# A hybrid recurrence-and-attention block: the second weight sum of three projection units is put behind two splits, and the next unit's first block behind one more load

## The chip, the core and the metric

The kernel runs on one core of a Trainium2 chip. The metric is the device time of one execution in microseconds (us), lower is better. The matrix engine TensorE is PE in the profile, the weight loads that overlap its matmuls are PEld, VectorE is DVE, ScalarE is ACT, GpSimd is POOL and SyncE is SP. SP issues the large loads on a queue of its own (SPq), POOL issues DMAs on another one.

## The reference, cut to what matters

```python
def rms_norm(x, w):
    y = x * lax.rsqrt(jnp.mean(x * x, axis=-1, keepdims=True) + EPS)
    return y * w

# x: (1, 256, 2048), all float32; one layer
z = rms_norm(h, norm_mix_w) @ w_in                       # 2048 x 11264
hq, hf, hi, hg, aq, ak, av, gates = jnp.split(z, ...)
y_a = hgrn2(hq, hf, hi, hg)                              # 8 heads of 128, gated recurrence over time
y_b = chunk_band_attention(aq, ak, av, rel_bias)         # 16 heads of 64, bias by relative distance
gate_a, gate_b = jnp.split(sigmoid(gates), 2)
merged = gate_a * (y_a @ w_branch_a) + gate_b * (y_b @ w_branch_b)
h = h + merged @ w_out
h = h + square(relu(rms_norm(h, norm_mlp_w) @ w_up)) @ w_down
return rms_norm(h, norm_final_w)
```

There are 256 tokens, so every weight is used once per token block and the work is a long row of matrix products with 256 rows.

## The kernel before, in words

**Arithmetic.** Products are made to float32 accuracy from two rounded parts of each operand. A weight piece is 128 x 1024 float32 (512 KB). ScalarE casts it into a high part (`wh`, line 91), VectorE subtracts that from the raw piece to get the low part (`wl`, line 92), and PE runs three matmuls, high by high, high by low, low by high (lines 135, 136 and 137, helper `mm3`). The function `parts` does the cast and the subtraction and appends the subtraction to the list `lows`. High and low parts sit in rings of four buffers each, and of five once the list `homes` has an entry "fifth", which is from the unit ga2 on. Instructions of a line in a helper all show that line, so tiles tell the units apart.

**Units.** A `Unit` makes a 256 x 1024 slice of a product with a 2048-deep contraction. Half of the depth (rows 0 to 7 of 16) is done with seven block products in place of eight, after Strassen and Winograd. The weight half has four blocks A, B, C, D of two pieces each. They are split and multiplied in this order: 11 with A, 22 with A, 12 with C, 11 with D, a plain piece, 21 with A, a plain piece, 21 with B, two plain pieces, 21 with D, plain pieces. Between them the blocks are changed in place: `sums("A","B")` adds B to A on VectorE (line 780) after the first product, `sums("A","C")` adds C to A before the 21 product with A, and `sent` makes POOL issue DMAs that add C to B and the changed A to D in SBUF (line 785). A DMA of `sent("D","A")` needs its D piece to have been split and its A piece to have been summed.

**Plain pieces.** The other half of the depth is eight plain pieces, `(n, (k, k+1))`, n being the column half. They are loaded into three buffers `rawp` in the order of `ITEMS`: (1,8), (1,10), (0,8), (0,10), and so on. So the fourth one, (0, (10, 11)), can be loaded only when the first one, (1, (8, 9)), has been split. The last two plain pieces of column half 1 are late: they are put into the list `late` and run inside the next unit, between its first products.

**Which units.** The projection uses `av` (attention values), `ga0` and `ga2` (first gate), `gb0` and `gb2` (second gate); later units are the output projection and the MLP. `alone` runs a unit and flushes its late pieces at once. It is called for `av` and for `ga0`, with `ga2` as the unit that follows `ga0`. So `av`, `ga0` and `ga2` begin with no late pieces in front of their second and third products, all others with two.

**Order.** The program is written as a list. A scheduler then places the instructions on each engine by priorities and estimated times; `tc.high_priority` pulls an instruction ahead, and `tc.issue_after(x)` keeps those in its block behind x. Every engine and every DMA queue then runs its list in order and waits where a semaphore is not yet there. The scores, the softmax and the value products of the attention (lines 587 to 626) are placed between the matmuls of units: those of the first eight heads start during `av`, those of the other eight run during `ga0`. In these, PE has three kinds of short float32 work: `s` (scores, 64-row operands, line 587), `tpp` (transposes of 128 x 128, line 610) and `pa` (value products, 64 columns, line 622). The pool of `s` has one buffer. During `ga0` the units' accumulators in PSUM are halves of pair tiles; from `ga2` on each one is a bank of its own.

**Lines named below.** 91 cast, 92 low part, 135 to 137 matmuls, 587 scores, 596 and 597 scores plus bias, 599 and 600 maxima, 606 and 607 scaling, 610 transposes, 688 loads of pieces, 123 loads of the qk projection's weights, 748 copies of an accumulator (`u`, and the start of one accumulator from another), 775 subtraction of `u`, 780 `sums`, 785 `sent`.

Before the change `sums("A","C")` is held behind the latest low part only in units made with `fresh=True`, which are `ga2` and `gb0`; in all units `then.load("A")` stands behind the copy `u1`:

```python
        u.product("11", "D", u.block(0, 1))
        with ExitStack() as es:
            if u.fresh:
                es.enter_context(tc.issue_after(lows[-1].ins))
            u.sums("A", "C")
        u.sent("D", "A")
        ...
        u1 = u.copy(token(f"u1_{u.what}"), "21")
        if then:
            then.load("A")
```

Of the kernel before, what the change touches and what calls it, by code (L numbers as in the profile page):

```python
# [22 lines left out]
NC = 512  # L23
# [10 lines left out]
C_HI, C_HG, C_AV = 0, HG, 2 * HG  # L34
# [16 lines left out]
def tile_hybrid_block(  # L51
# [5 lines left out]
    nc = tc.nc  # L57
# [42 lines left out]
    def new_act(what):  # L100

        return apool.tile([P, 4, 2, T], F32R, name=f"act_{what}", tag="act")
# [96 lines left out]
    xT = [new_act(f"x{c}") for c in range(4)]  # L199
# [3 lines left out]
    steps = [1, 1] + [2] * (KD // 2 - 1)  # L203
# [10 lines left out]
    done = [0, 0]  # L214
    for kt, n in zip(starts, steps):
        c, a = kt // 4, kt % 4
# [361 lines left out]
    def qk_chunk(col, what, factor, acc=None):  # L578
        return z_t(col, what, bp.tile([P, 2, T], F32, name=f"{what}T", tag="qk", bufs=6), factor, acc)
# [46 lines left out]
    def token(what, pool=None):  # L626
        if pool is not None:
            return pool.tile([P, NC], F32, name=what, tag="t2", bufs=8)
        return tk.tile([P, NC], F32, name=what, tag="t", bufs=TOK)

    def sigmoid(gate, acc, m):
        with tc.high_priority(offset=2000):
            nc.scalar.activation(gate, acc, AF.Sigmoid, scale=rstd[:, m:m + 1])
        return gate
# [46 lines left out]
    def piece(w, what, n0, k0, tag="raw"):  # L681

        pool, bufs = {"raw": (wpool, 6), "rawd": (xp, 2), "rawp": (xp, 3)}[tag]
        raw = pool.tile([P, 2 * NC], F32, name=f"{tag}_{what}", tag=tag, bufs=bufs)
        ncols = w.shape[-1]
        kpr = 4 * NC // ncols
        src = w[n0 // ncols:(n0 + NC) // ncols, k0 // kpr, :, k0 % kpr:k0 % kpr + 2, :].rearrange("c p a n -> p c a n")
        nc.sync.dma_start(raw.rearrange("p (c a n) -> p c a n", a=2, n=ncols), src)
        return raw, ncols < NC

    lows = []

    def parts(raw, what):

# [12 lines left out]
    def bank(what):  # L707
        if "banks" in homes:
            return homes["banks"].tile([P, NC], F32, name=f"acc_{what}", tag="k")
        row, col = what[-2:]  # L710
        if col not in pairs:
            pairs[col] = new_acc(what)
        return pairs[col][:, int(row) - 1, :]
# [6 lines left out]
    ITEMS = [(1, (8, 9)), (1, (10, 11)), (0, (8, 9)), (0, (10, 11)), (0, (12, 13)), (0, (14, 15))] + [(1, ks) for ks in LATE]  # L720

    class Unit:


        def __init__(self, lhs, S, w, n0, what, done, kt0=0, steps=lambda: (), start=5, fresh=False, tail=False):
            self.lhs, self.S, self.w, self.n0, self.what, self.done = lhs, S, w, n0, what, done
            self.kt0, self.make_steps, self.start, self.fresh, self.tail = kt0, steps, start, fresh, tail
            self.raw, self.c, self.items, self.steps = {}, {}, list(ITEMS), []

        def load(self, name):  # L730

# [4 lines left out]
        def load_item(self):  # L736

            n, ks = self.items.pop(0)
            self.raw[n, ks] = piece(self.w, f"{self.what}r{n}_{ks[0]}", self.n0 + n * NC, self.kt0 + ks[0], "rawp")

        def bank(self, i):

# [74 lines left out]
    def flush():  # L817
        while late:
            late.pop(0)()

    def run(u, then=None):

        def q():
            if late:
                late.pop(0)()

        def item(x):
            if x and x.items:
                x.load_item()

        if not u.raw:
            u.load("A")
            u.load("B")
            u.load("C")
            u.load("D")
        for _ in range(3 - sum(type(k) is tuple for k in u.raw)):
            item(u)
        at = iter(range(99))
        u.bank("11")
        u.product("11", "A", u.block(0, 0), True)  # L840
        u.begun("21", "11")
        q()
        u.sums("A", "B")
        u.sent("B", "C")
        item(u)
        u.bank("22")
        u.product("22", "A", u.comb(5), True)
        u.begun("12", "22")
        q()
        item(u)  # L850
        u.steps = list(u.make_steps())
        u.step(next(at))
        u.product("12", "C", u.comb(4))
        u.step(next(at))
        u.product("11", "D", u.block(0, 1))
        with ExitStack() as es:
            if u.fresh:
                es.enter_context(tc.issue_after(lows[-1].ins))
            u.sums("A", "C")
        u.sent("D", "A")  # L860
        u.step(next(at))
        u.plain(1, (8, 9))
        item(u)
        u.step(next(at))
        u.product("21", "A", u.comb(2))
        u1 = u.copy(token(f"u1_{u.what}"), "21")
        if then:
            then.load("A")
        u.step(next(at))
        u.plain(1, (10, 11))  # L870
        u.less("12", u1)
        item(u)
        u.step(next(at))
        u.product("21", "B", u.comb(7))
        u2 = u.copy(token(f"u2_{u.what}"), "21")
        if then:
            then.load("B")
            then.load("C")
        u.step(next(at))
        u.plain(0, (8, 9))  # L880
        u.less("22", u2)
        item(u)
        u.step(next(at))
        u.plain(0, (10, 11))
        item(u)
        u.step(next(at))
        u.product("21", "D", u.block(1, 1))
        if then:
            then.load("D")
        u.step(next(at))  # L890
        u.plain(0, (12, 13))
        item(u)
        u.step(next(at))
        u.plain(0, (14, 15))
        marks.clear()
        item(then)
        u.end(0)
        while u.steps:
            u.step(99)

        if u.tail:
            halves = [u.plain(1, ks, ()) for ks in LATE]
            for m, c in ((1, slice(0, T)), (0, slice(0, NC)), (1, slice(T, NC))):
                for h in halves:
                    h(m, c)
                u.done(m, 1, u.c["12"[m] + "2"], c)
            return

        def rest():
            u.plain(1, LATE[1])  # L910
            u.end(1)

        late.append(lambda: u.plain(1, LATE[0]))
        late.append(rest)


    Sx = {}
    for f in combos(xT, "x", tk, Sx):
        f()
    av = [[None] * NM for _ in range(2)]  # L920
# [5 lines left out]
    def alone(u, then=None):  # L926
        run(u, then)
        flush()
        pairs.clear()

    for g in range(2):
        qT = [qk_chunk(C_AQ + g * NC + i * T, f"aq{g}{i}", rstd8_t, None if g else acc_q[i]) for i in range(2)]
        kT = [qk_chunk(C_AK + g * NC + i * T, f"ak{g}{i}", rstd_t) for i in range(2)]
        if not g:
            alone(Unit(lambda: xT, lambda: Sx, w_in_n, C_AV, "av", values))
        yb.append(new_act(f"yb{g}"))
        pts = None
        for pr in range(5):
            last = pts
            if pr < 4:  # L940
                pts = attn_pair(g, pr, qT[pr // 2][:, pr % 2, :], kT[pr // 2][:, pr % 2, :])
            if last:
                attn_values(g, pr - 1, last, av[g])

    ga, gb = [], []
    units = []
    for gates, c, col, what, fresh in ((ga, 0, C_GA, "ga", False), (ga, 2, C_GA, "ga", True), (gb, 0, C_GB, "gb", True), (gb, 2, C_GB, "gb", False)):

        def done(m, n, acc, gates=gates, c=c, what=what):
            while len(gates) <= c + n:  # L950
                gates.append([None] * NM)
            gates[c + n][m] = sigmoid(token(f"gate_{what}{c + n}{m}", tkb if (what == "ga") == (c == 2) else None), acc, m)

        units.append(Unit(lambda: xT, lambda: Sx, w_in_t, col + c * NC, f"{what}{c}", done, fresh=fresh))
    alone(*units[:2])
    del units[0]
    bpool_cm.__exit__(None, None, None)
# [20 lines left out]
    for u, then in zip(units, units[1:] + [None]):  # L978
        run(u, then)
# [76 lines left out]
    def h_out(m, n, acc):  # L1056
        t = token(f"h1_{n}_{m}")
        with tc.high_priority(offset=2000):
# [9 lines left out]
    units = [Unit(lambda: mT, lambda: Sm, w_out, n0 * NC, f"wo{n0}", lambda m, n, acc, n0=n0: h_out(m, n0 + n, acc),  # L1068
                  steps=(lambda: h_blocks(0)) if n0 else (lambda: turned(mT, 3, "m3", ga)), start=2 if n0 else 0) for n0 in (0, 2)]
    fin = {}  # L1070
    for qd in range(NQ):
# [18 lines left out]
        for c in range(0, 4, 2):  # L1090
            def done(m, n, acc, c=c, rs=rs, qd=qd):
                t = token(f"r{qd}{c}{n}{m}")
                with tc.high_priority(offset=2000):
# [5 lines left out]
                              steps=(lambda turns=turns: turns(0)) if c else (lambda: ()) if qd else (lambda: h_blocks(2)), start=3 if c else 0))  # L1099
# [39 lines left out]
        for n0 in (0, 2):  # L1139
            units.append(Unit(lambda uT=uT: uT, lambda Su=Su: Su, w_down, n0 * NC, f"dn{qd}{n0}",  # L1140
                              lambda m, n, acc, *c, n0=n0, out_of=out_of: out_of(m, n0 + n, acc, *c), kt0=qd * KD,
                              steps=(lambda: ()) if n0 else (lambda turns=turns, last=last: turns(2) + [(3, finals)] * last),
                              start=0, tail=last and n0 == 2))

    for u, then in zip(units, units[1:] + [None]):
        run(u, then)
# [44 lines left out]
```

## Time and profile before

| | |
|---|---|
| median of 3 runs | 1399.73 us (1399.07 to 1400.38) |
| profiled execution, its own time | 1399.67 us |
| its span in the trace | 1398.0 us |
| mean granted TensorE clock | 0.998 |
| instructions | 18644 |
| read from HBM, written | 271.67 MB, 10.49 MB |

The profile is one execution. Its own time is 1.7 us more than its span, and 0.06 us under the median of the runs. In a timeline row the first number is the start in us from the beginning of the span, the second how long the row's instructions took together; what stands in square brackets is the idle time of the engine before it and what ended it. Rows of SPq and of POOL's DMA lines show the issue of a transfer and not its landing. In the chain of waits each row is a piece of the path that ended last, with its start, its length and what held it.

### The profile page before, as it was taken

The numbers are of one execution on the slowest core, as the hardware profiler recorded it, in microseconds if no ns is written. First come the engines' busy times: TensorE is split into PE (matmuls) and PEld (weight loads), VectorE is DVE, ScalarE is ACT, GpSimd is POOL, SyncE is SP. The second block draws the span as 40 slices with busy tenths as digits, with TensorE's granted clock in tenths as the row PEclk, the third lists the DMA queues.
The fourth block names the chain that finished last, engine by engine and source line by source line (L and its number), as shares of the span: only waits on it lengthen the run. The fifth ranks groups of instructions, "written<-read, shape, count | busy, mean of one in ns | idle before, by whom it ended". The sixth has DMA issues, their size and how long they took to land.

```text
span 1398.0 us, 18644 instructions
## 1 busy us (share of the span) xinstructions
PE 1381.4 (99%) x6550; PEld 1144.4 (82%) x6550; DVE 1138.2 (81%) x1431; ACT 922.3 (66%) x1192; POOL 143.8 (10%) x228
## 2 busy tenths in 40 slices
PE   9999999999999999999999999999999999999997
PEld 7889888878777888888888888888888888888885
DVE  7897997976978785687998987889877888879885
ACT  6774764665676674346777776778666876668764
POOL 2000001010100000001211001100011001010200
PEclk9999999999999999999999999999999999999999
DMA  9755455775769897658988889998899888999883
GB/s 318 242 168 161 154 166 181 225 269 162 183 187 271 251 278 225 193 169 268 283 244 275 252 268 267 274 280 240 249 295 299 248 230 254 281 279 275 267 245 114
DMA packets 124078, 331.62 MB, mean 237 GB/s; under 512 B 11072, under 2 KB 11840, under 8 KB 123600
## 3 DMA queue, kind: packets, MB, share of 16 engines
q1 hardware_dynamic: 103264, 264.80, 55.1%
q0 software_dynamic: 19568, 64.04, 23.3%
q10 hardware_dynamic: 1152, 1.60, 0.4%
q8 instruction: 51, 0.84, 0.2%
q14 instruction: 43, 0.35, 0.1%
HBM read 271.67 MB, written 10.49 MB: 202 GB/s over the span
## 4 chain that ended last, share of the span: by engine, by line
PE 90%; DVE 4%; DMA 3%; issue 1%; ACT 1%; POOL 0%; SPq 0%; POOLq 0%; ACTq 0%; DVEq 0%
PE acc_ak L177 2%; PE acc_aq L177 2%; PE acc_hf L177 2%; PE ps L414 1%; PE acc_ak L182 1%; PE acc_hq L177 1%; PE tp_u L108 1%; PE acc_ga0c L135 1%; PE acc_hg L136 1%; PE acc_bb L136 1%; PE acc_hg L135 1%; PE acc_ba L136 1%; PE acc_bb L137 1%; PE acc_ba L137 1%; PE acc_hg L137 1%
## 5 line engine op out<-in xcount | busy, mean ns | idle before, releaser
L177 PE MATMUL acc_hf<-act_x,wh_hf 128*128 128x512 f32 x128 | 41.0, 402 | 1.0 <-DVE f L190 1.0
L177 PE MATMUL acc_aq<-act_x,wh_aq 128*128 128x512 f32 x128 | 41.6, 406 | 0.0
L177 PE MATMUL acc_hq<-act_x,wh_hq 128*128 128x512 f32 x128 | 40.7, 399 | 0.0
L177 PE MATMUL acc_ak<-act_x,wh_ak 128*128 128x512 f32 x128 | 40.0, 396 | 0.1
L91 ACT CAST wh_bb<-raw_bb 128x1024 fp32r<-128x1024 f32 x16 | 16.9, 1054 | 23.3 <-PE acc_ba L137 17.7
L92 DVE TENSOR_TENSOR wl_bb<-raw_bb,wh_bb 128x1024 fp32r<-128x1024 f32 x16 | 19.6, 1223 | 14.8 <-ACT wh_bb L91 14.8
L91 ACT CAST wh_ba<-raw_ba 128x1024 fp32r<-128x1024 f32 x16 | 16.8, 1052 | 20.9 <-PE acc_bb L137 13.8
L92 DVE TENSOR_TENSOR wl_ba<-raw_ba,wh_ba 128x1024 fp32r<-128x1024 f32 x16 | 19.6, 1223 | 12.6 <-ACT wh_ba L91 12.6
L91 ACT CAST wh_aq<-raw_aq 128x1024 fp32r<-128x1024 f32 x16 | 16.8, 1050 | 19.0 <-PE acc_hg L137 8.8
L92 DVE TENSOR_TENSOR wl_aq<-raw_aq,wh_aq 128x1024 fp32r<-128x1024 f32 x16 | 19.6, 1223 | 11.4 <-ACT wh_aq L91 9.4
L182 PEld LDWEIGHTS acc_hq<-act_x,wl_hq 128*128 128x128 f32 x128 | 23.4, 188 | 6.1 <-DVE wl_hq L92 0.9
L182 PEld LDWEIGHTS acc_hf<-act_x,wl_hf 128*128 128x128 f32 x128 | 23.4, 188 | 6.1 <-DVE wl_hf L92 0.9
L182 PEld LDWEIGHTS acc_aq<-act_x,wl_aq 128*128 128x128 f32 x128 | 23.5, 188 | 5.4 <-issue 0.5
L182 PEld LDWEIGHTS acc_ak<-act_x,wl_ak 128*128 128x128 f32 x128 | 23.5, 188 | 5.3
L92 DVE TENSOR_TENSOR wl_hf<-raw_hf,wh_hf 128x1024 fp32r<-128x1024 f32 (+2 forms) x21 | 20.3, 967 | 7.8 <-ACT wh_hf L91 7.7
L91 ACT CAST wh_hf<-raw_hf 128x1024 fp32r<-128x1024 f32 (+1 forms) x19 | 16.9, 890 | 14.3 <-PE acc_hg L137 6.0
L182 PE MATMUL acc_aq<-act_x,wl_aq 128*128 128x256 f32 x128 | 25.9, 284 | 0.0
L92 DVE TENSOR_TENSOR wl_ak<-raw_ak,wh_ak 128x1024 fp32r<-128x1024 f32 x16 | 19.5, 1221 | 7.7 <-ACT wh_ak L91 7.7
L135 PE MATMUL acc_hi<-wh_hi,act_x 128*128 128x512 f32 x64 | 25.8, 403 | 0.0
L92 DVE TENSOR_TENSOR act_u<-tp_u,act_u 128x512 fp32r<-128x512 f32 x32 | 21.9, 685 | 4.7 <-ACT act_u L91 4.2
L135 PE MATMUL acc_hg<-wh_hg,act_x 128*128 128x512 f32 x64 | 25.7, 401 | 0.0
L1106 POOL DMA_DIRECT2D hd<-y x24 | 25.4, 1137 | 1.9 <-ACT y L1105 1.8
(1922 smaller groups left out, 5248.0 us busy)
## 6 DMA issues: line engine op xcount, KB each, us to landing
raw_hi<-in_w_in_n_dram SPq DMA_DIRECT2D x16, 512.0 KB, 4.4
raw_hg<-in_w_in_n_dram SPq DMA_DIRECT2D x16, 512.0 KB, 3.9
raw_aq<-in_w_in_t_dram SPq DMA_DIRECT2D x16, 512.0 KB, 4.3
raw_ak<-in_w_in_t_dram SPq DMA_DIRECT2D x16, 512.0 KB, 3.8
raw_ba<-in_w_branch_a_dram SPq DMA_DIRECT2D x16, 512.0 KB, 4.5
raw_bb<-in_w_branch_b_dram SPq DMA_DIRECT2D x16, 512.0 KB, 4.6
raw_hf<-in_w_in_t_dram SPq DMA_DIRECT2D x12, 512.0 KB, 3.9
raw_hq<-in_w_in_t_dram SPq DMA_DIRECT2D x12, 512.0 KB, 4.4
```

Source lines behind the costliest of these rows:

```text
L91: casts[:] = [(copy or nc.scalar.copy)(hi, src)]
L92: return nc.vector.tensor_tensor(lo, src, hi.bitcast(F32), op=ALU.subtract)
L108: nc.tensor.transpose(tp[:, j, :], src[:, j * P:(j + 1) * P], ident)
L135: nc.tensor.matmul(acc, hi, wh, start=first, stop=False, skip_group_check=True)
L136: nc.tensor.matmul(acc, hi, wl, start=False, stop=False, skip_group_check=True)
L137: nc.tensor.matmul(acc, lo, wh, start=False, stop=last, skip_group_check=True)
L177: nc.tensor.matmul(acc[:, cb, :], wh[:, cb * P:(cb + 1) * P], r.rearrange("p u t -> p (u t)"), start=kt == 0, stop=last)
L182: nc.tensor.matmul(acc[:, cb, 0:T], wl[:, cb * P:(cb + 1) * P], r[:, 0, :], start=False, stop=False)
L414: nc.tensor.matmul(ps[:, m, :], klf[:, a * P:(a + 1) * P], qrf[:, a * 192:(a + 1) * 192], start=True, stop=True)
L1106: nc.gpsimd.dma_start(hd[n][m], t, accum_op=ALU.add)
```

## The change

The change gives `Unit` a flag `lone`, set for `av`, `ga0` and `ga2`. In such a unit `sums("A","C")` is issued behind the last low part made so far, which is that of the second piece of D, so the order on VectorE is the splits of C and D first and the two additions then. `ga2` already had that from `fresh`. The load of the next unit's block A is issued behind the load of the plain piece (0, (10, 11)) of the unit itself; only `ga0` and `ga2` have a next unit at that place. To be able to name that load, `piece` keeps its last DMA in the list `loads` and `load_item` files it under the piece's name.

```diff
-        nc.sync.dma_start(raw.rearrange("p (c a n) -> p c a n", a=2, n=ncols), src)
+        loads[:] = [nc.sync.dma_start(raw.rearrange("p (c a n) -> p c a n", a=2, n=ncols), src)]
...
-    lows = []
+    lows, loads = [], []
...
-        def __init__(self, lhs, S, w, n0, what, done, kt0=0, steps=lambda: (), start=5, fresh=False, tail=False):
+        def __init__(self, lhs, S, w, n0, what, done, kt0=0, steps=lambda: (), start=5, fresh=False, lone=False, tail=False):
...
             self.raw[n, ks] = piece(self.w, f"{self.what}r{n}_{ks[0]}", self.n0 + n * NC, self.kt0 + ks[0], "rawp")
+            self.dma[n, ks] = loads[0]
...
         with ExitStack() as es:
-            if u.fresh:
+            if u.fresh or u.lone:
                 es.enter_context(tc.issue_after(lows[-1].ins))
             u.sums("A", "C")
         u.sent("D", "A")
...
         if then:
-            then.load("A")
+            with ExitStack() as es:
+                if u.lone:
+                    es.enter_context(tc.issue_after(u.dma[0, (10, 11)].ins))
+                then.load("A")
...
-            alone(Unit(lambda: xT, lambda: Sx, w_in_n, C_AV, "av", values))
+            alone(Unit(lambda: xT, lambda: Sx, w_in_n, C_AV, "av", values, lone=True))
...
-        units.append(Unit(lambda: xT, lambda: Sx, w_in_t, col + c * NC, f"{what}{c}", done, fresh=fresh))
+        units.append(Unit(lambda: xT, lambda: Sx, w_in_t, col + c * NC, f"{what}{c}", done, fresh=fresh, lone=what == "ga"))
```

In the built programs the order of PE's instructions differs in `ga0` alone, where the attention of the last eight heads is placed anew among the unit's matmuls; in `av` and `ga2` it is the same. VectorE's and ScalarE's orders differ in `ga0`, and VectorE's in `av` by the place of the two additions. The number of instructions is the same on every engine. On SP the load of (0, (10, 11)) moves ahead of two loads of the next unit in `ga0` and `ga2`, and later plain pieces move ahead of the next unit's blocks B, C and D; in `av` two plain pieces move ahead of one load each of the qk projection. On POOL, in `ga0`, two loads of bias and their two memsets move ahead of the `sent` from A to D.

More of the change, by code (lines that the diff above doesn't have):

```diff
@@ L722, in tile_hybrid_block @@
     class Unit:
-        def __init__(self, lhs, S, w, n0, what, done, kt0=0, steps=lambda: (), start=5, fresh=False, tail=False):
+        def __init__(self, lhs, S, w, n0, what, done, kt0=0, steps=lambda: (), start=5, fresh=False, lone=False, tail=False):
             self.lhs, self.S, self.w, self.n0, self.what, self.done = lhs, S, w, n0, what, done
-            self.kt0, self.make_steps, self.start, self.fresh, self.tail = kt0, steps, start, fresh, tail
-            self.raw, self.c, self.items, self.steps = {}, {}, list(ITEMS), []
+            self.kt0, self.make_steps, self.start, self.fresh, self.lone, self.tail = kt0, steps, start, fresh, lone, tail
+            self.raw, self.dma, self.c, self.items, self.steps = {}, {}, {}, list(ITEMS), []
         def load(self, name):
```

## The prediction

> **What bounds the kernel now.** I read the page first, then PE's waits, the chain of waits, and the timelines of the three units that the change touches.
>
> ```profile
> span 1398.0 us, 18644 instructions
> PE 1381.4 (99%) x6550; PEld 1144.4 (82%) x6550; DVE 1138.2 (81%) x1431; ACT 922.3 (66%) x1192; POOL 143.8 (10%) x228
> ```
>
> PE is busy in 99% of the span. An edit that moves no PE work can win only PE's idle time, 16.6 us in all, and the slow places inside its busy time; it can lose without limit by a new wait. In PE's waits one row of over half a us lies in the units that change:
>
> ```profile
> PE acc_ga2c L135 <- ACT u_ga L748: 1.1, 1, 1.1
> ```
>
> The bound of 0.2% used below, about what a measurement of this kernel can tell from no change, is 2.8 us. The idle time in reach is less than that.
>
> **ga2: the late fourth piece.** The chain of waits shows what stands behind the 1.1 us:
>
> ```profile
> 425.97 1.15 DVE wl_ga2r L92
> 427.13 10.89 DMA rawp_ga2r<-in_w_in_t_dram
> 439.05 1.63 ACT wh_ga2p21D L91 x2
> 440.94 0.58 ACT u_ga L748
> 441.57 0.50 PE acc_ga2c L135
> 442.07 0.23 PE acc_ga2c L136
> ```
>
> The piece (0, (10, 11)) is issued at 427.13, as soon as the first plain piece is split, and lands 10.89 us later, at 438.02. ScalarE's queue holds behind its cast two casts of D and the copy `u`, and PE must not overwrite the copied accumulator before 441.53. The stall is 1.1 us idle and a restart of 0.50 instead of 0.23, so 1.4 us. Without it PE would come to this matmul at about 440.3. From landing to matmul the chain takes 441.57 - 438.02 = 3.55, so a landing by 436.75, 9.6 us after issue, hides all of it.
>
> Why 10.9 us: two loads of the next unit stand ahead of it in the same queue, and the two `sent` transfers from A to D are in flight.
>
> ```profile
> 424.89 1.50 SPq L688 DMA_DIRECT2D raw_gb0A<-in_w_in_t_dram  x2
> 427.13 0.37 SPq L688 DMA_DIRECT2D rawp_ga2r<-in_w_in_t_dram  x1
> ```
>
> The change puts the piece first. Its issue can't come earlier, since its buffer comes free when the split of the chain's first row ends (425.97 + 1.15), but nothing stands ahead of it. The nearest rows are two fourth pieces that were issued with both `sent` transfers in flight and no load of the last 3 us still ahead of them, in ga0 and av (each answer: the issue, then the landing):
>
> ```profile
> L688 SPq DMA_DIRECT2D rawp_ga0r<-in_w_in_t_dram x1: 367/367/367, 373.1 to 373.1; - x1
> DMA to landing us min/median/max: 8.0/8.0/8.0
> L688 SPq DMA_DIRECT2D rawp_avr<-in_w_in_n_dram x1: 328/328/328, 273.0 to 273.0; - x1
> DMA to landing us min/median/max: 8.5/8.5/8.5
> ```
>
> 8.0 to 8.5 is under 9.6, so the stall goes: -1.4 us (bounds -1.4 and 0, if the landing stays at 10.9). What is late next is the pieces (0, (12, 13)) and after; they too move ahead of gb0's blocks on SP, and gb0's A, moved back by 1 us, is not cast before ga2's own pieces are.
>
> **av: the same lateness is brought in.** Here the additions were early; now they come behind D's splits.
>
> ```profile
> 261.81 1.22 DVE L780 TENSOR_TENSOR raw_avA<-raw_avA,raw_avC 128x1024 f32<-128x1024 f32 x1
> 265.54 1.22 DVE L92 TENSOR_TENSOR wl_avp12C<-raw_avC,wh_avp12C 128x1024 fp32r<-128x1024 f32 x1
> 266.68 1.22 DVE L780 TENSOR_TENSOR raw_avA<-raw_avA,raw_avC 128x1024 f32<-128x1024 f32 x1
> 267.81 1.22 DVE L92 TENSOR_TENSOR wl_avp12C<-raw_avC,wh_avp12C 128x1024 fp32r<-128x1024 f32 x1
> 268.95 2.35 DVE L92 TENSOR_TENSOR wl_avp11D<-rawd_avD,wh_avp11D 128x1024 fp32r<-128x1024 f32 x2
> 271.79 1.23 DVE L92 TENSOR_TENSOR wl_avr<-rawp_avr,wh_avr 128x1024 fp32r<-128x1024 f32 x1 [0.48 <-ACT wh_avr L91]
> ```
>
> PE gains nothing from the earlier splits, it runs this stretch without a wait. What moves is the DMA. Each raw buffer of C has two last readers, the split and the addition; in before the split is last, and SP issues the first two loads of the qk projection into these buffers right behind the two splits (266.76 and 269.03):
>
> ```profile
> 266.79 2.60 SPq L123 DMA_DIRECT2D raw_aq<-in_w_in_t_dram  x2
> 273.04 0.33 SPq L688 DMA_DIRECT2D rawp_avr<-in_w_in_n_dram  x1
> ```
>
> Afterwards the addition is last. With one addition less ahead of them, D's low parts end at about 270.7, the additions at 271.8 and 273.0, the first plain piece's low part at 274.1 (each 1.14 from start to start, as above). So the two raw_aq loads are issued at 271.8 and 273.0, the `sent` transfers at about 272.1 and 273.2, and the fourth piece at 274.1. That is ga2's pattern of before to a quarter of a us: loads 2.24 and 1.10 us ahead, transfers in flight. Two such pieces were measured, 10.9 us in ga2 and this one in gb0, also behind two loads:
>
> ```profile
> 466.05 1.51 SPq L688 DMA_DIRECT2D raw_gb2A<-in_w_in_t_dram  x2
> ```
>
> ```profile
> L688 SPq DMA_DIRECT2D rawp_gb0r<-in_w_in_t_dram x1: 368/368/368, 468.4 to 468.4; - x1
> DMA to landing us min/median/max: 10.1/10.1/10.1
> ```
>
> 10.1 to 10.9 puts the landing at 284.2 to 285.0. When is it needed?
>
> ```profile
> 282.71 1.05 ACT L91 CAST wh_avr<-rawp_avr 128x1024 fp32r<-128x1024 f32 x1 [1.18 <-PE acc_avc L137]
> 284.07 1.06 ACT L91 CAST wh_avp21D<-rawd_avD 128x1024 fp32r<-128x1024 f32 x1 [0.30 <-PE acc_avc L137]
> 285.43 0.58 ACT L748 COPY u_av<-acc_avc 128x512 f32<-128x512 f32 x1 [0.30 <-PE acc_avc L137]
> ```
>
> ```profile
> 286.07 0.50 PE L135 MATMUL acc_avc<-wh_avr,act_x 128*128 128x512 f32 x1
> ```
>
> ScalarE's queue casts the fourth piece, then D, then copies `u`, and PE's matmul at 286.07 waits for that copy. Two casts (0.96 each from start to start, by ga2's chain), 0.07 of waiting and 0.64 from the copy's start to the matmul make 2.6, so a landing after 283.45, 9.35 us from issue, delays PE one for one: 0.75 to 1.55 us. Bounds: 0 at 8.5 us, 1.6. I take +1.2, by the two rows with the same pattern.
>
> [...] The two landings of 10.1 and 10.9 decide for me.
>
> **ga0: attention placed anew.** Here VectorE is full:
>
> ```profile
> 362.00:385.00 23.00, 22.70 (x108) 16.38 (x105) 22.19 (x44) 17.22 (x32) 3.69 (x7) 1.00 0.81 206
> ```
>
> After PE's and the weight loads' columns comes VectorE's, busy for 22.19 of 23.00 us. Moving 2.4 us of additions makes room for softmax work, and PE's order changes. Some of before's groups are costly. Eight `s` and three `tpp` interleaved:
>
> ```profile
> 381.73 0.42 PE s L587 x4
> ...
> ...
> 384.06 0.43 PE acc_ga0c L137
> ...
> 390.84 0.33 PE tpp L610 x3
> ...
> 392.10 0.85 PE s L587 x8
> ```
>
> From 381.73 to 384.06, that is 2.33, and with a restart of 0.2 (the 0.43 at 384.06 against a usual 0.23) 2.53; apart, 0.33 and 0.85 with the same restart, 1.38. The new order has them apart: -1.15. It joins two groups of `pa` that stood apart, one restart less (-0.2). The other mixed or split groups change places, one for one. Two waits:
>
> ```profile
> 368.29 0.58 ACT acc_ga0c L748
> 368.91 0.50 PE acc_ga0c L135
> ```
>
> This wait of 0.6 for ScalarE's copy is replaced, as three matmuls of 11 stand there now in place of one. New: PE needs D's first low part. By VectorE's rows (a low part 1.14, the scores' additions and maxima 0.2 to 0.33 each) the softmax steps placed ahead move it from 368.5 to 368.9, its end to 370.1, while PE, now with the second `s` group before it, wants it at 369.4: 0.7. That group waits 0.2 for the single buffer of scores. The transposes placed behind 21 with B wait 0.7 for a scaling that now stands behind a low part of D, and smaller ones add 0.3: 1.9 in all. The same adding-up along before's order gives 1.6 where PE's rows show 0.7, so I take 1.3. ga0 together: -1.15 - 0.2 - 0.6 + 1.3 = -0.65. Bounds: -1.95 with no new wait, 0 with all 1.9; dearer only if a DMA is late (below). The moved fourth piece: issued at 376.2 after the later split, at 8.0 us lands at 384.2, cast at 384.9. POOL's `sent` to D comes later by 4 us, landing at about 380 and 384, and D is cast from 386 on. The memsets ahead of it wait for bias that lands at 372.5, before the addition ends at 373.9 (both estimates, from the same walk).
>
> **The sum.** -1.4 - 0.65 + 1.2 = -0.85, against 1399.67: 1398.8 us, and by the 0.06 between that execution and the median, 1398.9. Nothing else on PE moves; all later units keep their order and merely start earlier.
>
> **Rivals.** *Slower: the transfers from A to D hold the fourth piece everywhere.* If it lands 10.9 us after issue also where it stands first, ga2 wins nothing (427.13 + 10.9 = 438.0); av pays 1.6; in ga0 it lands at 387.1, 2.2 after its cast would start, and an exponential, a scaling and the transposes behind it wait as long: -0.65 + 2.2 = +1.55. Together +3.1, 1402.8. It decides from 8.7 us in ga0, 9.35 in av, 9.6 in ga2. For: 10.1 and 10.9 measured. Against: 8.0 and 8.5 for pieces with free queues.
>
> *Faster: av's piece lands in time, and ga0 has no new waits.* Then -1.4 - 1.95 = -3.35, 1396.4. For: av's piece took 8.5 in before, and what stands ahead of it afterwards, loads of raw_aq, is not what stood ahead of ga2's. Against: VectorE in ga0 is full, so some wait is likely.
>
> *No effect: the stalls change places.* In ga2 the next wait (D's casts, whose ring frees late) takes 0.5 to 1.4 of the gain, and ga0's new waits eat its order's gain: about 1400.0 with av's cost.
>
> **How the numbers follow.** Forecast 0.48, the slower rival 0.17, the faster 0.2, no effect 0.15. Range: it reaches to the faster rival, and up to the terms' upper bounds with ga0 a little dearer, leaving out the slower rival: 1396.3 to 1401.8. Faster by over 0.2% (below 1396.9) is the faster rival, 0.2; slower (above 1402.5) the slower one, 0.17; the rest is within, 0.63.
>
> **What would show it.** Right: no wait of PE for u_ga in ga2, the piece's landing there under 9.6 us; a new wait before u_av's copy, behind a cast that waits for rawp_avr, with that landing over 9.35 us; in ga0 from the first matmul to the last some 54.3 us instead of 54.9, with a wait for wl_ga0p11D. Wrong: av without a stall (the landings' analogy fails), ga0 longer than 55 us (the walk of VectorE's queue), or any unit after ga2 with a wait that it has not now.

## The result, and the profile after

The changed kernel takes 1400.92 us (median of 22 runs, 1398.2 to 1404.3), the kernel before 1399.01 us in the same 22 rounds. The ratio is 1.0014 with a 95% interval from 1.0008 to 1.0020: by this ratio the change costs 1.96 us, where the prediction had it win 0.85.

The profiled execution after has a span of 1398.8 us. PE's waits in the stages that change (line and tile, what released it; total, times and longest in us; rows from other stages are left out) name the places:

```profile
PE tpp L610 <- DVE sb L606: 1.7, 1, 1.7
PE acc_avc L135 <- ACT u_av L749: 0.8, 1, 0.8
PE acc_avc L136 <- DVE wl_avr L92: 0.7, 1, 0.7
PE acc_ga0c L136 <- DVE wl_ga0p11D L92: 0.6, 1, 0.6
PE s L587 <- DVE sb L597: 0.5, 1, 0.5
```

The row of `acc_ga2c` is gone, as forecast, and so is the wait for `acc_ga0c`. In their place stand the wait for `u_av` and that for D's low part in ga0, both forecast; the transposes' wait in ga0, 1.7 where the walk had 0.7; and two that no step had, a second one in av (for `wl_avr`) and one in the projection that follows av (`s`).

In av the fourth plain piece (issue, then landing) and the two transfers from A to D (landings: shortest, median, longest; the second one is the longest) were, after:

```profile
L688 SPq DMA_DIRECT2D rawp_avr<-in_w_in_n_dram x1: 328/328/328, 273.2 to 273.2; - x1
DMA to landing us min/median/max: 10.1/10.1/10.1
...
L786 POOL DMA_DIRECT2D rawd_avD<-raw_avA x2: 847/848/849, 271.4 to 272.6; - x2
DMA to landing us min/median/max: 7.9/9.2/10.5
```

The piece took 10.1 us, inside the forecast of 10.1 to 10.9, and ScalarE's queue stood behind it:

```profile
283.37 1.05 ACT L91 CAST wh_avr<-rawp_avr 128x1024 fp32r<-128x1024 f32 x1 [2.77 <-DMA rawp_avr<-in_w_in_n_dram]
284.32 1.04 ACT L91 CAST wh_avp21D<-rawd_avD 128x1024 fp32r<-128x1024 f32 x1
285.27 0.58 ACT L749 COPY u_av<-acc_avc 128x512 f32<-128x512 f32 x1
```

In ga0 the chain of waits (start, length, what) shows the largest loss. The piece was issued at 377.7 and landed 9.9 us later:

```profile
L688 SPq DMA_DIRECT2D rawp_ga0r<-in_w_in_t_dram x1: 368/368/368, 377.7 to 377.7; - x1
DMA to landing us min/median/max: 9.9/9.9/9.9
```

```profile
387.65 0.12 ACT wh_ga0r L91
387.77 0.83 issue
388.60 0.60 ACT sb L603 x2
389.20 0.95 ACT wh_ga0p21D L91
390.15 0.02 issue
390.17 1.23 DVE wl_ga0p21D L92
391.40 0.21 DVE sb L606
391.61 0.14 issue
391.74 0.61 PE tpp L610 x3
```

Read upwards: PE's transposes wait for a scaling, the scaling stands on VectorE behind a low part of D, that waits for D's cast on ScalarE, which stands behind an exponential and behind the cast of the piece that had just landed.

In ga2 the piece stood first in its queue and took 9.6 us. PE did not wait there:

```profile
L688 SPq DMA_DIRECT2D rawp_ga2r<-in_w_in_t_dram x1: 367/367/367, 429.1 to 429.1; - x1
DMA to landing us min/median/max: 9.6/9.6/9.6
```

One profile is one execution, and the spans of both kernels wander by some us. So the experiments are read by stages, each worked out from PE's timeline: av from its first to its last matmul; from there to ga0's first; from there to ga2's first; from there to gb0's first. "Piece" is the time from the issue of the unit's fourth plain piece to its landing, "wait" PE's wait that follows from it (for `u` in av and ga2, of the transposes for `sb` in ga0).

| us | av | piece, wait | to ga0 | ga0 | piece, wait | ga2 | piece, wait |
|---|---|---|---|---|---|---|---|
| before | 42.76 | 8.5, 0 | 57.52 | 54.10 | 8.0, - | 37.32 | 10.9, 1.1 |
| after | 44.51 | 10.1, 0.8 | 57.99 | 54.79 | 9.9, 1.7 | 36.04 | 9.6, 0 |
| after2 (the changed kernel again) | 43.83 | 10.4, 1.1 | 58.22 | 53.85 | 8.9, 0.8 | 36.39 | 10.0, 0.2 |

### The profile page after: what moved, and what is told of

Its sections match the earlier page's. It is cut to its first block, busy times and chain, and to the rows that moved or that the text cites. A ratio compares the mean times of both kernels' runs of the same rounds, so it can differ in the third digit from the quotient of the medians.

```text
span 1398.8 us, 18647 instructions
## 1 busy us (share of the span) xinstructions
PE 1380.9 (99%) x6550; PEld 1144.5 (82%) x6550; DVE 1138.2 (81%) x1431; ACT 923.7 (66%) x1192; POOL 143.9 (10%) x228
## 4 chain that ended last, share of the span: by engine, by line
PE 88%; DVE 5%; DMA 4%; issue 2%; ACT 1%; POOL 0%; POOLq 0%; SPq 0%; ACTq 0%; DVEq 0%
PE acc_ak L177 2%; PE acc_aq L177 2%; PE acc_hf L177 2%; DMA raw_hf<-in_w_in_t_dram 2%; DMA rawp_avr<-in_w_in_n_dram 1%; PE ps L414 1%; PE acc_ak L182 1%; PE acc_hq L177 1%; PE tp_u L108 1%; PE acc_bb L137 1%; PE acc_bb L135 1%; PE acc_hg L136 1%; PE acc_hg L135 1%; PE acc_ba L137 1%; PE acc_hg L137 1%
## 5 line engine op out<-in xcount | busy, mean ns | idle before, releaser
L91 ACT CAST wh_ak<-raw_ak 128x1024 fp32r<-128x1024 f32 x16 | 16.8, 1051 | 13.1 <-PE acc_ak L177 6.9
L98 POOL TENSOR_TENSOR ro<-ms,mhalf 128x2 f32<-128x2 f32 x8 | 5.9, 737 | 189.8 <-DVE ms L97 189.8
```

Of the source, the lines that this page charges most:

```text
L91: casts[:] = [(copy or nc.scalar.copy)(hi, src)]
L98: nc.gpsimd.tensor_tensor(dst, ms, mhalf[:, :width], op=ALU.pow)
```

## The experiments

**One unit at a time.** The flag `lone` was given to one unit only:

```diff
-            alone(Unit(..., "av", values, lone=True))      # only_ga0, only_ga2
+            alone(Unit(..., "av", values))
-        units.append(Unit(..., fresh=fresh, lone=what == "ga"))
+        units.append(Unit(..., fresh=fresh, lone=False))                         # only_av
+        units.append(Unit(..., fresh=fresh, lone=what == "ga" and not fresh))    # only_ga0
+        units.append(Unit(..., fresh=fresh, lone=what == "ga" and fresh))        # only_ga2
```

> The change made for av alone; ga0 and ga2 as before. Theory A (each unit pays for itself; the fourth plain piece lands 0.2 to 1.8 us after the second transfer from A to D, and the loads that were held back leave the last plain pieces late): av from first to last matmul 44.5 us against 42.8, with waits of about 0.8 (u_av) and 0.7 (wl_avr), from there to ga0's first matmul 58.0 against 57.5, ga0 54.1 and ga2 37.3 as before; +2.2 us, ratio 1.0016. Theory B (the loss belongs to ga0, av's waits only shift with the run): av below 43.2, ratio 1.000.

> The change made for ga0 alone. Theory A: av and ga2 as before, from ga0's first matmul to ga2's first 54.8 us against 54.1, with a wait of some 1.7 us of the transposes for a scaling behind a low part of D; +0.7 us, ratio 1.0005. Theory B (ga0's late piece was backlog of transfers that the changed av left behind): no such wait, 54.1 - 0.65 = 53.4, ratio 0.9995.

> The change made for ga2 alone, which is only the order of the loads on SP there. Theory A: from ga2's first matmul to gb0's first 36.0 us against 37.3, all else as before; -1.3 us, ratio 0.9991. Theory B (the gain is given back in the units behind it): 36.0 here but 1.3 more until gb2's end, ratio 1.000.

| us | ratio, 95% interval | av | to ga0 | ga0 | ga2 |
|---|---|---|---|---|---|
| only_av | 1.0009, 1.0000 to 1.0017 | 44.39 | 57.54 | 54.12 | 37.30 |
| only_ga0 | 1.0006, 0.9997 to 1.0015 | 42.80 | 57.53 | 54.05 | 36.95 |
| only_ga2 | 0.9992, 0.9983 to 1.0000 | 42.80 | 57.52 | 55.29 | 36.32 |

Theory A holds for av's length and for ga2; gb0 to the end of gb2 takes 87.27 us in every profile, so nothing of ga2's gain is given back there. In only_av the whole loss is one wait, with the piece at 10.9 us; the wait for `wl_avr` and the longer way to ga0, which theory A had too, did not come:

```profile
PE acc_avc L135 <- ACT u_av L749: 1.7, 1, 1.7
```

For ga0 neither expectation fits: the profile has a wait of 0.8 in place of 1.7, and no loss. But that profile is the fastest of the kernel's 12 executions (1397.49 us, their median is 1400.25), so it does not speak for the others. And only_ga2, in which ga0 has its old order, lost 1.2 us in ga0. PE's wait and VectorE's timeline there:

```profile
PE tpp L610 <- ACT wh_ga0r L91: 1.2, 1, 1.2
```

```profile
398.65 0.29 DVE L596 TENSOR_TENSOR sb<-s,bias 128x128 f32<-128x128 f32 x1 [1.83 <-POOL bias L594]
```

The first row names a cast of ScalarE, but what the transposes at 400.00 read is scaled by VectorE, and that scaling ended at 399.86, queued behind an addition that had waited 1.83 us for a bias. POOL's memset, which the addition waited for, had itself waited for that bias to land, at 398.42. So here a bias that landed late held VectorE and then the transposes, and ga0 varies in both orders: over six profiles with the old order it took 54.10 to 55.29, mean 54.54.

**What makes the piece late: the loads ahead of it, or the transfers from A to D?** Two kernels with the change for av alone, one profile each. In av_q_behind the first two loads of the qk projection are also held behind the fourth piece; in av_no_sent the transfers from A to D are left out.

```diff
+                with ExitStack() as es:
+                    if what == "aq10" and k0 < 8:
+                        es.enter_context(tc.issue_after(av_unit[0].dma[0, (10, 11)].ins))
                 (nc.scalar if k0 + a < beside else nc.sync).dma_start(...)        # av_q_behind
...
-        u.sent("D", "A")
+        if u.what != "av":
+            u.sent("D", "A")                                                       # av_no_sent
```

> The change made for av alone, and in addition the two loads of the qk projection that stood ahead of the fourth plain piece are issued behind it. Theory A (the piece lands with the second transfer from A to D, whatever stands ahead of it): landing 0.2 to 1.8 us after that transfer, at 281.5 to 283.3 (counted from the span's start, with the span's head as in the profile after), a wait for u_av of 0 to 0.8 us that is gone only so far as the transfer itself comes earlier; the last plain pieces late as before, wait for wl_avr 0.7 or more. Theory B (the loads ahead in the same queue make it late): landing 5 to 6 us after issue, at about 279, no wait for u_av.

> The change made for av alone, with av's two transfers from A to D left out (so the product 21 with D is made with a D that lacks the changed A). Theory A (the fourth plain piece lands with the second of these transfers, which take longer when loads run beside them): without them it lands 5 to 7 us after its issue although two loads of the qk projection still stand ahead of it; no wait for u_av, av 42.8 us in place of 44.4. Theory B (the loads ahead in the same queue hold it): still 10 to 11 us, wait for u_av 0.8 to 1.7, av 43.6 to 44.5.

```profile
L691 SPq DMA_DIRECT2D rawp_avr<-in_w_in_n_dram x1: 328/328/328, 274.1 to 274.1; - x1
DMA to landing us min/median/max: 7.8/7.8/7.8
...
L789 POOL DMA_DIRECT2D rawd_avD<-raw_avA x2: 849/850/852, 272.4 to 273.5; - x2
DMA to landing us min/median/max: 4.4/6.3/8.3
```

(The added lines shift the line numbers by three.) In av_q_behind the piece had nothing ahead of it in its queue and still took 7.8 us, not the 5 to 6 of theory B: it landed at 281.96, 0.2 us after the second transfer (273.49 + 8.27). But that transfer itself took 8.3 us, against 10.5 in the changed kernel and 11.4 in only_av, where the two loads are issued just ahead. They were in flight beside it here too, for SP issued them right behind the piece:

```profile
274.55 1.64 SPq L126 DMA_DIRECT2D raw_aq<-in_w_in_t_dram  x2
```

In av_no_sent the loads were ahead again, the transfers were missing, and the piece took 6.6 us:

```profile
L688 SPq DMA_DIRECT2D rawp_avr<-in_w_in_n_dram x1: 328/328/328, 272.6 to 272.6; - x1
...
DMA to landing us min/median/max: 6.6/6.6/6.6
```

av took 42.77 us in both, with no wait. So the piece lands behind the second transfer from A to D, and the two loads lengthen that transfer by 2 to 3 us (10.5 and 11.4 against 8.3) when they are issued just ahead of the transfers, and not when they are issued behind the piece. Over the three units before and after, the piece landed 0.2 to 1.8 us behind the second transfer, over all profiles 0.2 to 2.6. That loads ahead of the piece count through the transfer alone is not shown: the 6.6 us of av_no_sent are more than the 4.5 us of ga0_no_sent below, which has neither transfers nor loads just ahead, but in another unit. Theory A's other part fell: the wait for `wl_avr` did not come in av_q_behind, though those loads were later still.

**The same in ga0.** ga0_no_sent leaves ga0's transfers out; ga0_sums and ga0_load do one half of the change for ga0 each. Each has one profile.

```diff
+        if u.what != "ga0":
             u.sent("D", "A")                                                       # ga0_no_sent
...
-                if u.lone:
+                if False:
                     es.enter_context(tc.issue_after(u.dma[0, (10, 11)].ins))       # ga0_sums
...
-            if u.fresh or u.lone:
+            if u.fresh:
                 es.enter_context(tc.issue_after(lows[-1].ins))                     # ga0_load
```

> The change made for ga0 alone, with ga0's two transfers from A to D left out (so its product 21 with D lacks the changed A). Theory A: the fourth plain piece lands 5 to 6.5 us after its issue in place of 8.8 to 9.9, the transposes' wait of 0.8 to 1.7 us goes, ga0's first matmul to ga2's first 53.3 us in place of 54.05 and 54.8. Theory B (the transposes wait because VectorE is full, not because of the piece): the wait stays, 54.0 to 54.8.

> Half of the change for ga0 alone: the additions behind D's splits, with the new order of attention on PE that comes with it, but ga2's block A loaded where it was, ahead of the fourth plain piece. Theory A (loads beside the transfers lengthen the second one, and the piece lands with it): piece 10 to 11 us after its issue, the transposes' wait 1.7 to 2.8 us, ga0 55 to 56 us. Theory B (ga0's new waits come from VectorE's order alone): as with the whole change for ga0, 54.0 to 54.8.

> The other half for ga0 alone: only ga2's block A is loaded behind the fourth plain piece; the engines' orders are those of before. Theory A: nothing in ga0 waited for that piece, so ga0 stays as it is in other executions with that order, 54.1, or 55.1 to 55.3 where a bias load ends late; ga2's A still lands some 25 us ahead of its use. Theory B (the loads' place is what changes ga0's time): 53.5 or less, or over 55.5.

In ga0 the orders of PE, VectorE and ScalarE are the same in all kernels of this table, so the transposes' wait can be set against the piece alone:

| kernel | issue to landing of the piece | wait of the transposes | ga0 |
|---|---|---|---|
| ga0_no_sent | 4.46 | 0.35 | 53.38 |
| only_ga0 | 8.83 | 0.78 | 54.05 |
| after2 | 8.89 | 0.78 | 53.85 |
| after | 9.86 | 1.71 | 54.79 |
| ga0_sums | 10.67 | 2.56 | 55.56 |

From 8.83 on the wait grows one for one with the landing, above 8.1 us. ga0_sums shows what the second half of the change is for in ga0: with ga2's block A still ahead of it, the piece takes 10.7. ga0_load took 54.11, as before. Against it, ga0_no_sent's 53.38 puts the new order on PE at 0.7 us better when nothing is late.

**The rest.** Three kernels that put parts together: the changed kernel with av_q_behind's edit (change_mended), the change for both ga units (ga_both), and ga2's part with each bias load of ga0 issued ahead of the memset of the bias before it (ga2_bias), which changes POOL's order alone:

```diff
-        bias = bp.tile([P, T], F32, name=f"bias{hd}", tag="bias", bufs=3)
-        nc.gpsimd.dma_start(bias, ...)
-        nc.gpsimd.memset(bias[0:CH, 0:CH], NEG)
+        for i in range(hd, hd + 2 if hd % 8 < 7 else hd + 1):
+            if i not in biases:
+                biases[i] = bp.tile([P, T], F32, name=f"bias{i}", tag="bias", bufs=3)
+                bias_dma[:] = [nc.gpsimd.dma_start(biases[i], ...)]
+        bias = biases[hd]
+        with ExitStack() as es:
+            if hd >= 8:
+                es.enter_context(tc.issue_after(bias_dma[0].ins))
+            nc.gpsimd.memset(bias[0:CH, 0:CH], NEG)
```

> The changed kernel once more, for a second profile of it. Theory A (av +1.7 with what follows it, ga0 on average as before because its new order's gain is paid back by the transposes' wait, ga2 -0.9): av 44.3 to 44.5, ga0 54.0 to 55.0, ga2 36.0 to 36.4; in all +0.8 to +1.5 us, ratio 1.0005 to 1.0011. Theory B (ga0 too is longer with the change in most executions): ga0 54.8 or more again, +1.5 to +2.5, ratio 1.0011 to 1.0018.

> The whole change, and the two loads of the qk projection held behind av's fourth plain piece. Theory A (av's loss comes from those two loads running beside the transfers from A to D, which then end later, and the piece with them): av 42.8 us, second transfer 8 to 9 us long in place of 10.5 to 11.4; ga0 54.0 to 55.0, ga2 36.0 to 36.4; in all -0.3 to -1.3 us, ratio 0.9991 to 0.9998. Theory B (the additions' later place alone costs av its time): av 44, ratio 1.0005 or more.

> ga2's part of the change alone, and each of ga0's loads of bias issued ahead of the memset of the bias before it, in place of behind it. Theory A (in some executions of the order of before a bias that lands late holds the transposes for 0.5 to 1.2 us, because each load of bias waits for the memset and so the landing of the one before): no wait of the transposes over 0.2 us in ga0, ga0 54.1, ga2 36.0 to 36.4; -1.3 us against the mean of before, ratio 0.9991. Theory B (bias is late because the transfers are congested, and an earlier issue does not help): ga0 54.1 to 55.3 as before.

> The change for ga0 and ga2, av as before. Theory A: av 42.8, ga0 54.0 to 55.0 with the transposes' wait growing one for one with the time from the fourth piece's issue to its landing above 8 us, ga2 36.0 to 36.4. Theory B (ga0's transposes wait by something else): the wait does not follow the landing.

| us | ratio, 95% interval | av | to ga0 | ga0 | its wait | ga2 |
|---|---|---|---|---|---|---|
| after2 | 1.0014, 1.0003 to 1.0025 | 43.83 | 58.22 | 53.85 | 0.8 | 36.39 |
| change_mended | 0.9999, 0.9988 to 1.0009 | 42.75 | 57.53 | 54.81 | 1.8 | 36.63 |
| ga2_bias | 0.9991, 0.9981 to 1.0000 | 42.75 | 57.53 | 54.09 | 0 | 35.92 |
| ga_both | one time | 42.75 | 57.51 | 56.33 | 1.8 | 36.03 |

change_mended has av back at 42.75, with the second transfer at 8.3 us: av's loss comes from those two loads. Its ratio is just over the 0.9991 to 0.9998 expected and its ga2 over the 36.4. after2 has theory B's ratio but shorter av and ga0 than either theory; its profile is 1.6 us under the median of its executions. ga_both brought something new. Its wait is that of after, 1.8 us, but ga0 is 1.5 us longer. The windows show why (after the length of the window: busy PE, PEld, DVE, ACT, POOL with counts; granted clock, DMA share, GB/s):

```profile
388.00:390.00 2.00, 0.62 (x4) 0.59 (x5) 2.00 (x5) 1.20 (x2) 0.23 (x1) 0.96 1.05 407
390.00:392.00 2.00, 2.00 (x6) 1.52 (x6) 1.93 (x5) 1.36 (x5) 0.00 (x0) 0.50 1.04 408
392.00:394.00 2.00, 2.00 (x8) 1.57 (x7) 1.48 (x6) 0.49 (x2) 0.68 (x2) 0.68 1.05 408
394.00:396.00 2.00, 2.00 (x16) 1.34 (x14) 0.79 (x3) 1.46 (x3) 0.00 (x0) 1.00 1.05 409
```

After 1.83 us without work, PE's granted clock is 0.50 for some 3.4 us, and eight matmuls come 0.43 us apart in place of 0.23. Whether this belongs to the wait was tried with the longest wait and the shortest, and ga2_bias was run again:

> The half of the change with the longest wait in ga0 (2.6 us), timed. Theory A (a wait of over about 1.7 us sometimes halves the TensorE clock for some 3.4 us, 1.6 us lost): mean granted clock 0.996 or less in a third of the runs or more, ratio 1.0010 to 1.0016 where the profiled stage alone (55.56 against a mean of 54.54) gives 1.0007. Theory B (the clock has nothing to do with it): low clocks as rare as in before (1 in 16), ratio 1.0007.

> The change for ga0 with its transfers from A to D left out (its product 21 with D lacks the changed A), timed: the engines' orders are those of ga0_sums_t, the wait is 0.35 us. Theory A: no run at a clock of 0.996 or less, or one, ratio 0.9990 to 0.9994. Theory B: low clocks as often as in ga0_sums_t.

> ga2_bias once more: ratio 0.9991 again, all runs at 0.997 or more, ga0 54.1 with no wait of the transposes, ga2 35.9 to 36.4.

The profile of ga0_sums_t shows the drop again, on PE's timeline, and ga0 took 57.25 us in place of 55.56:

```profile
390.44 0.73 PE L610 MATMUL tpp<-ident,sb 128*128 128x128 f32 x3 [2.75 <-DVE sb L606]
390.82 0.78 PE L135 MATMUL acc_ga0c<-wh_ga0r,act_x 128*128 128x512 f32 x1
391.39 0.63 PE L136 MATMUL acc_ga0c<-wl_ga0r,act_x 128*128 128x512 f32 x1
391.82 0.63 PE L137 MATMUL acc_ga0c<-wh_ga0r,act_x 128*128 128x512 f32 x1
```

Its ratio is 1.0018 (1.0009 to 1.0027), more than theory A's 1.0010 to 1.0016, and far over the 1.0007 of its first stage time; ga0_no_sent_t has 0.9994 (0.9985 to 1.0003) and no drop in its profile, as theory A has it; a bias was late there (2.41 us of VectorE's idle time) and ga0 took 54.38, so late bias belongs to the new order too. Low mean clocks were fewer than forecast, 3 of 11 runs in ga0_sums_t and 1 of 11 in ga0_no_sent_t. This count can miss some: 3.4 us at half clock take 0.0012 off the mean (3.4 x 0.5 / 1398), which from 0.998 can leave 0.997. ga2_bias2 has 0.9992 (0.9983 to 1.0001), ga0 54.11 without a wait of the transposes, and ga2 36.59, over the 36.4 expected.

The lowest ratios are those of ga2's part of the change, alone (0.9992) and with the bias loads one earlier (0.9991 and 0.9992). All three intervals end at about 1.000, so the gain over before is likely and not settled; over the changed kernel, by the ratios to before, it is some 3 us. What the earlier bias adds is not shown by these times. Its two profiles have no wait of the transposes, where three of the six with the old order have one of 0.5 to 1.2 us.

## Why the prediction was wrong, step by step

All three terms came out dearer than forecast: ga2 by 0.7 us, av by 0.7 and ga0 by 0.9. With any one of them as forecast the sum would still be a loss. They share a step, the landing of the fourth piece: its length from issue to landing was taken from another unit, in ga0 from the old order, where the runs show that the piece lands behind the second transfer from A to D. The step that failed most is ga0's, where no gain came.

**ga2, -1.4: right in kind, half the size on average.** The wait went because the piece landed earlier, and it decides at 9.8 us (10.48 gives 0.7, 10.89 gives 1.1), where the step had 9.6 (it has PE ready at 440.3, PE's idle time begins at 440.47). But the piece did not land after 8.0 to 8.5; with the load first it took 9.2 to 10.2, so in some executions 0.2 to 0.4 us of wait stays. And before's profile was at the high end: over ten profiles without the change ga2 took 36.51 to 37.32, mean 37.00; over seven with it 35.92 to 36.63, mean 36.27. That is -0.73.

**av, +1.2: right in place and size, and not the whole.** The forecast wait for `u_av` was 0.75 to 1.55; it came with 0.8, 1.1 and 1.7, beyond 9.3 us of landing as the step said (9.35). What was missed is what comes behind it. av and the stretch to ga0 together took 102.50, 102.05 and 101.93 against 100.28: +1.9 on average. In after the last plain piece of av and a bias were late too (0.7 and 0.5). Why these two come in some executions is open: the delay of the loads alone does not bring them (av_q_behind). The reason that the step gave for 10.9 us was half right. The two loads matter, but largely because they lengthen the second transfer from A to D, behind which the piece lands: in av that transfer took 9.1 us in before and 10.5 in after, and after's piece landed 0.2 us after it. With the same two loads behind the piece the transfer took 8.3 us (av_q_behind).

**ga0, -0.65: the step that failed.** Much of it held: with nothing late the new order gains 0.7 us (ga0_no_sent's 53.38 against the shortest time of the old order), and the wait for D's first low part was 0.6 (0.7 forecast). The transposes' 0.7 held as well, so long as the piece took under 8.9 us (0.78). The failing term is the moved fourth piece, "issued at 376.2 after the later split, at 8.0 us lands at 384.2". The issue was right: counted from ga0's first matmul it came after 13.9 us, forecast were 13.7 (376.2 less 362.53; the 377.7 of the profile after is later because ga0 itself began 1.3 us later). The 8.0 us failed: the piece took 9.9, in other profiles of the whole change for ga0 8.8 to 9.9. The transfers from A to D come later in this unit, as forecast, and the piece's issue moves less: it is now 0.6 us behind the second one, before 1.4 us, and the piece lands 1.6 to 2.0 us after that transfer, before 1.3 us. So of the 0.8 to 1.9 us that it takes longer, 0.8 is the closer issue. The slower rival had the right chain for ga0 ("an exponential, a scaling and the transposes behind it wait as long") but set its point at 8.7 in place of 8.1, and tied it to a loss in ga2 that did not come. The sign of being wrong, ga0 over 55 us, came (its count begins 0.8 us before ga0's first matmul, so 54.79 is 55.6 there), though by the piece and not by VectorE's own queue. Over five profiles the new order took 53.85 to 56.33, mean 54.77, against 54.54.

**What no step had: the price of a long wait.** PE was taken to lose the time that it waits and a short restart. The drop of the clock adds 1.4 to 1.5 us on top of the longer wait in ga_both (against after) and in ga0_sums_t (against ga0_sums). These are two of the three profiles with a wait over 1.8 us; in ga0_sums a wait of 2.56 brought none, nor did those of 1.67, 1.71 and 1.76 in only_av, after and change_mended. In the changed kernel itself no profile caught it. There it is inferred: the two profiles with a drop are the only ones with a mean granted clock of 0.996, and 13 of the changed kernel's 34 timed runs are at 0.996 or below, of before 5 of 85; those 13 are on average 1.6 us longer than the others.

**The sum.** From the means of the stages, +1.9 - 0.7 + 0.2 = +1.4 us, with one drop in five profiles of ga0's new order; the timed ratio is worth 1.1 to 2.8 us. Some 0.3 us of the difference may lie in drops that are more frequent than one in five (an estimate: 13 of 34 less one in five, at 1.5 us each). The rest is not assigned; the profiles of after and after2 are 0.4 and 1.6 us under the medians of their kernels' runs.

## What to carry to other kernels

A load that was issued just behind the accumulating transfers landed 0.2 to 2.6 us after the last of them. To judge such a load, count what was issued in the last us ahead of those transfers, on another queue too: two loads there, on SP's queue where the transfers are on POOL's, cost av's piece 2 to 3 us (10.1 to 10.9 us against 7.8), the same two loads right behind the piece did not. A landing time borrowed from another place is worth something only if the same transfers are at the same stage there, and where the answer turns on 1 us, one profile is not enough to hold it. And a wait of PE near 2 us is not priced by its length: in these runs a wait of up to 1.76 us cost its length, and of the three longer ones those of 1.83 and 2.75 us cost 1.4 to 1.5 us more, that of 2.56 us did not.

## What the hardware showed beyond that

After waits of 1.83 us (ga_both) and 2.75 us (ga0_sums_t) PE's granted clock was 0.50 for 3.41 us. After the waits of 1.67 to 1.76 us, and even after that of 2.56 us in ga0_sums, it was not halved, so it is not the length alone. These are windows of 3.41 us around the wait, in ga_both, in after and in ga0_sums (columns as above; PE's busy time is the first after the length):

```profile
386.45:389.86 3.41, 1.58 (x9) 1.01 (x8) 3.26 (x7) 2.75 (x5) 0.70 (x2) 1.00 1.04 401
389.86:393.27 3.41, 3.41 (x11) 2.63 (x10) 3.34 (x10) 1.86 (x7) 0.14 (x1) 0.50 1.05 407
...
389.19:392.60 3.41, 1.70 (x9) 1.15 (x8) 3.20 (x8) 2.62 (x5) 0.70 (x2) 1.00 1.04 399
...
385.17:388.58 3.41, 2.19 (x13) 1.29 (x13) 1.53 (x3) 2.75 (x5) 0.68 (x2) 1.00 1.03 347
388.58:391.99 3.41, 2.07 (x11) 1.74 (x11) 3.34 (x9) 2.52 (x7) 0.03 (x1) 1.00 1.03 382
```

In ga_both PE was idle for 1.83 us of the first window, and the clock is 0.50 in the whole of the second, in which PE has no idle time: it dropped at 389.86, 0.48 us after PE had gone on at 389.38. In after PE was idle for 1.71 us of its window, in ga0_sums for 1.22 and 1.34 us of its two, all at a clock of 1.00; in both profiles it is also 1.00 from 392 to 400. ga0_sums and ga0_sums_t have the same order on PE and waits of 2.56 and 2.75 us, one without a drop and one with it. What decides beside the length is not shown.
